# State-space chunks in quarter steps, six leading half tiles, and latent attention with hi and lo apart

## The chip, the core and the metric

The kernel runs on one core of a Trainium2 chip. The metric is the device time of one execution in microseconds (us); the core works with TensorE (matrix products, PE in the rows), VectorE (DVE), ScalarE (ACT), GpSimd (POOL) and the DMA queues, of which SP's carries most transfers.

## What is computed

Two stacks of layers on 512 positions of 1024 features, in float32. The first has two layers of a feed-forward block, a mixer, another feed-forward block and a gated embedding; the change doesn't touch it. The second has four branches, each between two norms: a state-space branch, a window attention, a latent attention and a gating unit (SGU).

```python
def s5_branch(h, ...):            # 64 groups of 16 channels, 64 states each
    u, z = split(h @ w_in)
    bu = einsum('blgh,gph->blgp', u, b)             # complex
    s = scan(a, bu)                                 # s[t] = a * s[t-1] + bu[t]
    y = gelu(real(einsum(s, c)) + d_skip * u)
    y = y * sigmoid(y @ w_glu + b_glu)
    return (y * silu(z)) @ w_out

def mla_branch(h, ...):           # 16 heads
    c_q, c_kv, k_rope, z = split(h @ w_in)          # 768, 256, 32, 1024
    q = rmsnorm(c_q) @ w_uq                         # 96 a head, 32 of them rotated
    k, v = rmsnorm(c_kv) @ w_ukv                    # 64 + 64 a head
    o = causal_softmax(q k^T) @ v
    return (o * silu(z)) @ w_out

x = x + rmsnorm(branch(rmsnorm(x)))
```

## The kernel before

Activations lie transposed: a tile is 128 features x 512 positions. Every float32 operand of a product is kept as two parts, hi and lo, and a product is three matmuls, hi x hi, hi x lo and lo x hi, into one PSUM bank (`mm3`, L446). A tile of a projection (`mtile`, L460) is up to 8 k steps of `mm3`. Weights come in units of 8 blocks of 128 x 128 (512 KB) by SP's queue into three buffers (`_dma`); `_split` (L394) makes hi on ScalarE and lo on VectorE, two units ahead of their use. Units of the four output projections are kept in SBUF slots, since they are used twice.

The order of the work is written out by hand. After k steps 2, 4 and 6 of a tile, and once after the tile, the program calls `fine` (L572) or `step` (L556); `step` counts a tick, advances the generators in `bgs`, and then calls `fine`, which runs what `soon` has put off and advances the generators in `fines`. So a generator in `bgs` moves twice a tile and one in `fines` four times, a quarter tile apart. All engines take their instructions in the order of this program. `split_soon` (L616) puts off the lo half of a split to the next `fine`, `split` (L605) does both at once; `join` (L635) copies one half of a product's rows on ScalarE and later adds the other on VectorE.

`lead` (L475) starts a projection whose last operands are not ready: it does the first `a` k steps of `m` tiles one tile after the other, calling `fine` after each second k step and `step` after each tile, and then one k step after the other for all `m` tiles, waiting for the operand where needed. Each tile in it had its own bank, and later tiles of the lead held their look-ahead of weight splits back (`hold`). `post_out` (L1265) is the output projection of a branch with the norm behind it, by halves of 256 positions: the first half of all 8 tiles with a lead of 3 half tiles and OUT_LEAD[i] k steps (state-space, window, latent, SGU), then the second half with the kept weights.

The state-space stage (`s5`, L1559): 16 tiles of the input projection (u, then z); each u tile goes through DRAM by two SP DMAs into another layout. The generator `ssm` (L1624) works on 8 chunks: `scan_in` (L1574, TensorE products, two ScalarE copies out of the same bank, eight VectorE operations with the scan among them), `scan_out` (L1598, TensorE products, a copy, two SP DMAs through DRAM) and `finish` (L1614, the skip term, gelu and split into the operand of the GLU projection). In `bgs`, steps half a tile apart: chunks 3 apart, lags 3, 6 and 10. Tables for the scan come by POOL's queue two chunks ahead (`tabs`, L1546).

The latent attention (`mla`, L1877): `latent` makes the compressed operands; then for 8 pairs of heads come two query tiles of 6 k steps, one key tile of 2 k steps, and for every second pair four pieces of V in two banks (`split_v`). The key tile's halves are copied by SP DMAs to the heads' key slots, and a pair is `ready` three ticks later. `causal` (L1049), a generator in `fines`, does for each head scores, exp, divide, transposes (`turn`), their lo parts and the product with V (`pv`), at lags of 9, 10, 11 and 13 calls; heads start at least 4 calls apart. V's hi and lo stood packed in one operand of 128 columns for a head, so `pv` was two matmuls a block (`mm2`, L455) and its result had to be joined from two halves of the rows.

## Time and profile before

| | |
|---|---|
| median of 3 runs | 3344.68 us (3342.61 to 3346.49) |
| the profiled execution | 3344.01 us |
| its span | 3342.2 us |
| TensorE, VectorE, ScalarE, GpSimd busy | 97%, 63%, 39%, 13% |
| mean granted TensorE clock | 0.988 |

The stages of the second stack lie at about 2318 to 2500 us (state-space and GLU), 2500 to 2565 (its output projection), 2565 to 2720 (window attention), 2720 to 2790 (its output projection), 2790 to 3027 (latent operands and attention), 3027 to 3140 (output projection, the first part with the last heads beside it) and 3140 to 3342 (SGU). An engine's idle time matters where it is TensorE's, and the releaser named beside a wait is the instruction that ended it. L248 is the line through which all VectorE instructions go, so these are told apart by their tiles and shapes.

### The profile page before, as it was taken

Reading aid. Unit: us, or ns where it says so; the run is one execution under the profiler, and the core shown is the slowest. Engines: PE = TensorE matmul, PEld = TensorE weight load, DVE = VectorE, ACT = ScalarE, POOL = GpSimd, SP = SyncE. Lnnn points to the kernel's source line nnn. Section 1 sums busy time; section 2 is a strip of 40 time slices with the busy share of each in tenths; the row PEclk is TensorE's granted clock in tenths of the full one; section 3 lists DMA queues with packets and bytes.
Section 4 is the critical chain, followed back from the end, with each engine's and each line's share of the span. In section 5 each row is a group of like instructions: output and inputs, shape, how many; then the busy total and the mean of one; then the engine's idle time right before and its main releaser. Section 6 shows DMA issues by size and latency. Waiting matters only on the chain. (4 is left out here: it accounts for less than half of the span.)

```text
span 3342.2 us, 42393 instructions
## 1 busy us (share of the span) xinstructions
PE 3249.7 (97%) x15832; PEld 2704.9 (81%) x15832; DVE 2107.2 (63%) x4096; ACT 1313.9 (39%) x2242; POOL 440.8 (13%) x558
## 2 busy tenths in 40 slices
PE   9999999999999999999999999999999899998997
PEld 7888777888888888887778888887879788877887
DVE  6653488766653676536887654347665876676665
ACT  4322334433322333323434423234444764455432
POOL 0100013001100011000220000001103332143201
PEclk9999999999999999999999999999999999998998
DMA  5433221224432334332222332334623122322221
GB/s 179 134 113 101 88 95 64 95 89 136 140 119 95 94 130 139 114 99 91 89 64 95 106 119 95 119 127 150 210 91 105 58 77 83 108 66 64 82 82 64
DMA packets 120302, 348.08 MB, mean 104 GB/s; under 512 B 30560, under 2 KB 33280, under 8 KB 120096
## 3 DMA queue, kind: packets, MB, share of 16 engines
q1 hardware_dynamic: 103824, 295.68, 27.7%
q0 software_dynamic: 16272, 49.69, 4.4%
q8 instruction: 125, 2.05, 0.2%
q14 instruction: 81, 0.66, 0.1%
HBM read 312.75 MB, written 28.11 MB: 102 GB/s over the span
## 5 line engine op out<-in xcount | busy, mean ns | idle before, releaser
L450 PE MATMUL mm<-s,whi 128*128 128x512 f32 (+1 forms) x3528 | 1381.0, 391 | 17.0 <-ACT s L777 7.1
L452 PE MATMUL mm<-s,wlo 128*128 128x512 f32 (+1 forms) x3528 | 1364.0, 387 | 5.9 <-DVE wlo L248 5.9
L451 PE MATMUL mm<-s,whi 128*128 128x512 f32 (+1 forms) x3528 | 1364.8, 387 | 3.7 <-DVE s L248 3.3
L248 DVE TENSOR_TENSOR wlo<-raw,whi 128x1024 fp32r<-128x1024 f32 (+1 forms) x488 | 594.0, 1223 | 534.3 <-ACT whi L407 530.8
L450 PEld LDWEIGHTS mm<-s,whi 128*128 128x128 f32 x3528 | 665.8, 189 | 151.8 <-ACT s L777 7.5
L452 PEld LDWEIGHTS mm<-s,wlo 128*128 128x128 f32 x3528 | 665.0, 188 | 144.9 <-DVE wlo L248 9.9
L451 PEld LDWEIGHTS mm<-s,whi 128*128 128x128 f32 x3528 | 665.9, 189 | 134.9 <-DVE s L248 8.2
L407 ACT CAST whi<-raw 128x1024 fp32r<-128x1024 f32 (+1 forms) x488 | 508.1, 1045 | 557.6 <-PE mm L451 275.8
L248 DVE TENSOR_TENSOR s<-s,s 128x512 f32<-128x512 f32 (+8 forms) x920 | 454.5, 519 | 147.4 <-ACT s L608 77.7
L248 DVE TENSOR_TENSOR s<-mm,rbc 128x512 f32<-128x512 f32 x296 | 199.6, 686 | 193.4 <-PE mm L452 172.2
L1081 POOL TENSOR_SCALAR s<-s,m 128x128 f32<-128x128 f32 (+3 forms) x128 | 157.1, 1233 | 502.0 <-DVE m L248 292.8
L248 DVE SCALAR_TENSOR_TENSOR s<-s,vecs,s 128x511 f32<-128x511 f32 (+13 forms) x256 | 181.3, 749 | 4.9 <-DMA s<-yd 3.0
L608 ACT CAST s<-s 128x512 fp32r<-128x512 f32 (+1 forms) x125 | 75.4, 613 | 266.3 <-DVE s L248 266.3
L884 ACT ACTIVATE s<-s 128x512 f32<-128x512 f32 x88 | 55.6, 632 | 251.6 <-DVE s L248 251.6
L450 PE MATMUL mm<-s,s 128*128 128x256 f32 x448 | 131.7, 294 | 11.8 <-ACT s L618 5.1
L777 ACT ACTIVATE s<-h,vecs 128x512 fp32r<-128x512 f32 (+1 forms) x112 | 70.9, 633 | 182.4 <-DVE h L248 182.4
L451 PE MATMUL mm<-s,s 128*128 128x256 f32 x448 | 129.7, 289 | 1.3 <-DVE s L248 1.0
L452 PE MATMUL mm<-s,s 128*128 128x256 f32 x448 | 129.2, 288 | 0.2 <-DVE s L248 0.2
L248 DVE TENSOR_TENSOR s<-sd,s 128x512 fp32r<-128x512 f32 (+5 forms) x186 | 93.9, 530 | 54.1 <-ACT s L1089 36.0
L248 DVE SCALAR_TENSOR_TENSOR s<-h,vecs,s 128x512 fp32r<-128x512 f32 (+1 forms) x112 | 80.5, 721 | 65.9 <-ACT s L777 65.9
L450 PE MATMUL sd<-s,whi 128*128 128x512 f32 x296 | 120.7, 408 | 0.9 <-ACT whi L407 0.9
L452 PE MATMUL sd<-s,wlo 128*128 128x512 f32 x296 | 116.2, 393 | 2.8 <-DVE wlo L248 2.8
(216 smaller groups left out, 3402.9 us busy)
## 6 DMA issues: line engine op xcount, KB each, us to landing
raw<-in_mix_dram SPq DMA_DIRECT2D x104, 512.0 KB, 3.5
raw<-in_ff2i_dram SPq DMA_DIRECT2D x88, 512.0 KB, 3.5
raw<-in_ff1i_dram SPq DMA_DIRECT2D x87, 512.0 KB, 3.6
raw<-in_ff1o_dram SPq DMA_DIRECT2D x44, 512.0 KB, 3.5
raw<-in_ff2o_dram SPq DMA_DIRECT2D x44, 512.0 KB, 3.5
raw<-in_mlaw_dram SPq DMA_DIRECT2D x33, 512.0 KB, 3.5
tab<-s POOLq DMA_DIRECT2D x64, 256.0 KB, 2.3
s<-tab POOLq DMA_DIRECT2D x64, 256.0 KB, 5.7
```

What stands on the lines that cost most here:

```text
L248: return f(*a, **kw)
L407: self.nc.scalar.copy(hi.bitcast(F32R), src)
L450: mm(ps, wh, xh, start=first, stop=False)
L451: mm(ps, wh, xl, start=False, stop=False)
L452: mm(ps, wl, xh, start=False, stop=last)
L608: nc.scalar.copy(hi.bitcast(F32R), src)
L777: self.nc.scalar.activation(hi.bitcast(F32R), src, AF.Copy, scale=gv)
L884: nc.scalar.activation(sg, ta, AF.Silu)
L1081: nc.gpsimd.tensor_scalar(out=pr[:, c], in0=pr[:, c], scalar1=ri, scalar2=None, op0=ALU.mult)
```

## The change

- The state-space generator moves from `bgs` to `fines`; chunks are 5.5 quarter steps apart (alternately 5 and 6). `scan_in` is cut in three: the products, copies and the first vector product (lag 7), two vector operations and the scan with two copies (8), the turn back with three operations (9); scan-out follows at 13, finish at 20. The next tables are asked for after the third part.
- In `lead` with a column range, two half tiles share a bank (only the first matmul in a bank starts it), and the look-ahead of weight splits isn't held back. `post_out` leads with 6, 6, 6 and 3 half tiles, by 5, 6, 5 and 4 k steps, and takes its 8 result slots one by one.
- In the latent attention V's hi and lo are two operands, each with the 128 columns of two heads; `pv` is `mm3`, 12 matmuls a head instead of 8, and only the head's own 64 rows of the result are used, without a join. V's four pieces are split one a call. `split` takes the place of `split_soon` for latent, query, key and result tiles.

```diff
-S5_LAGS = 10, 6, 3, 3
+S5_LAGS = 20, 13, 9, 8, 7
+S5_STEPS = 5.5
-OUT_LEAD = 4, 6, 4, 4
+OUT_LEAD = 5, 6, 5, 4
+OUT_TILES = 6, 6, 6, 3
@@ lead
+        banks = [self.mm() for _ in range((m + 1) // 2)] if c is not None else []
...
-                x, o = (x[0][:, c], x[1][:, c]), o[:, :c.stop - c.start]
-            self.mm3(o, w[j][k], x, k == 0, k == nk - 1)
+                x = x[0][:, c], x[1][:, c]
+            self.mm3(o, w[j][k], x, k == 0 and (c is None or j % 2 == 0), k == nk - 1 and (c is None or j % 2 == 1 or j == m - 1))
         for j in range(m):
-            pss.append(self.mm())
-            w.append([self.block(hold=j * nk // UB) for _ in range(nk)])
+            pss.append(self.mm() if c is None else banks[j // 2][:, j % 2 * 256:(j % 2 + 1) * 256])
+            w.append([self.block(hold=j * nk // UB if c is None else 0) for _ in range(nk)])
@@ post_out
-        ys = self.slots(KD)
+        ys = []
...
+                if e == 0:
+                    ys.append(self.slot())
...
-        for m, ps in enumerate(self.led(M, KD, KD, 3, halves[0], OUT_LEAD[i])):
+        for m, ps in enumerate(self.led(M, KD, KD, OUT_TILES[i], halves[0], OUT_LEAD[i])):
@@ s5
-            vt, x, m8 = self.slot(), self.slot(), M8.pop(m)
-            c, s = a[2:]
+            vt, x = self.slot(), self.slot()
...
+            S[m] = vt, x
+
+        def scan(m):
+            (vt, x), m8, s = S[m], M8[m], tables[m][0][3]
             v.tensor_tensor(g3(x)[:, :, 1:], g3(x)[:, :, 1:], g3(s)[:, :, 1:], op=ALU.mult)
             v.tensor_tensor(g3(vt)[:, :, 1:], g3(vt)[:, :, 1:], g3(x)[:, :, 1:], op=ALU.add)
             v.tensor_tensor_scan(x, m8, vt, 0.0, op0=ALU.mult, op1=ALU.add)
             for r, q in ((top, bot), (bot, top)):
                 nc.scalar.copy(m8[r], x[q])
-            v.tensor_tensor(vt, x, c, op=ALU.mult)
-            v.scalar_tensor_tensor(out=m8, in0=m8, scalar=-1.0, in1=s, op0=ALU.mult, op1=ALU.mult)
+
+        def turned(m):
+            (vt, x), m8, a = S[m], M8.pop(m), tables[m][0]
+            v.tensor_tensor(vt, x, a[2], op=ALU.mult)
+            v.scalar_tensor_tensor(out=m8, in0=m8, scalar=-1.0, in1=a[3], op0=ALU.mult, op1=ALU.mult)
             v.tensor_tensor(vt, vt, m8, op=ALU.add)
             self.free(m8, x, a)
             S[m] = vt
@@ ssm
-            d = S5_LAGS[3]
-            for k in range(d * (KD - 1) + S5_LAGS[0] + 1):
-                while len(UG) <= min(k // d, KD - 1):
+            jobs = {}
+            for m in range(KD):
+                for n, (f, lag) in enumerate(zip((finish, scan_out, turned, scan, scan_in), S5_LAGS)):
+                    jobs.setdefault(int(S5_STEPS * m) + lag, []).append((n, f, m))
+            for k in range(max(jobs) + 1):
+                while len(UG) <= min(int(k / S5_STEPS), KD - 1):
                     yield
...
+                for _, f, m in sorted(jobs.get(k, []), key=lambda x: x[0]):
+                    f(m)
+                    if f is turned:
+                        self.tabs(m + 1 + S5_AHEAD)
...
-                self.bgs.append(bg)
+                self.fines.append(bg)
@@ mla
-                    self.split_soon(t, hi, lo, self.vec(gname, m), lambda: (self.free(t), out.append((hi, lo))))
+                    self.split(t, hi, lo, self.vec(gname, m))
                     self.stat_add(st, t)
+                    self.free(t)
+                    out.append((hi, lo))
...
-            w = [x[:, c].bitcast(F32R) for x in V[h // 4]]
+            vh, vl = self.r(V[h // 4])
+            c = [slice(j % 2 * 256 + p % 2 * P, j % 2 * 256 + (p % 2 + 1) * P) for j in range(4)]
             def epi():
-                t = self.slot()
-                def rest():
-                    v.tensor_tensor(Z[p][rows], Z[p][rows], t[rows], op=ALU.mult)
-                    self.free(t)
-                    if h % 2:
-                        x = self.slot(), self.slot()
-                        self.split_soon(Z[p], *x, None, lambda: (self.free(Z[p]), M.append(x)))
-                self.join(t[rows], po, rest)
+                v.tensor_tensor(Z[p][rows], Z[p][rows], po[rows], op=ALU.mult)
+                if h % 2:
+                    M.append((self.slot(), self.slot()))
+                    self.split(Z[p], *M[p])
+                    self.free(Z[p])
...
-                         lambda h: None, score, values, MLA_LAGS, self.mm2)
+                         lambda h: None, score, values, MLA_LAGS, self.mm3)
...
-                    for src, two, r in xs:
-                        nc.scalar.activation(two[:, 0].bitcast(F32R), src, AF.Copy, scale=r)
-                    for i, (src, two, r) in enumerate(xs):
-                        if i % 2 == 0:
-                            yield
-                        v.scalar_tensor_tensor(out=two[:, 1].bitcast(F32R), in0=src, scalar=r, in1=two[:, 0],
-                                               op0=ALU.mult, op1=ALU.subtract)
+                    for i in range(4):
+                        yield
+                        c = slice(i % 2 * 256, (i % 2 + 1) * 256)
+                        self.split(vps[i // 2][:, c], hl[0][i // 2][:, c], hl[1][i // 2][:, c],
+                                   box["kvc"][:, i:i + 1])
...
-                    self.split_soon(t, hi, lo, None, lambda: self.free(t))
+                    self.split(t, hi, lo)
+                    self.free(t)
...
-                def rest():
-                    while len(scored) < 2 * p - 2:
...
-                self.split_soon(t, *tt, None, rest)
+                self.split(t, *tt)
+                while len(scored) < 2 * p - 2:
+                    self.fine()
+                for h in (2 * p, 2 * p + 1):
+                    for a, b in zip(KS[h % 4], tt):
+                        nc.sync.dma_start(a[nope(h)], b[nope(h)])
+                    ready[h] = self.tick
+                self.free(t, tt)
```

## Rows read from the trace of the kernel before

**Rows 1.** The page, busy time, share of the span and instructions of TensorE first.
```profile
PE 3249.7 (97%) x15832; PEld 2704.9 (81%) x15832; DVE 2107.2 (63%) x4096; ACT 1313.9 (39%) x2242; POOL 440.8 (13%) x558
```

**Rows 2.** Windows by stretch: length, busy us of each engine, granted clock, DMA.
```profile
core 0: us, PE busy (x) PEld busy (x) DVE busy (x) ACT busy (x) POOL busy (x), PEclk, DMA share, GB/s
2318.00:2381.80 63.80, 59.11 (x343) 51.48 (x341) 39.20 (x59) 32.05 (x42) 9.96 (x19) 1.00 0.77 237
2381.80:2395.40 13.60, 13.60 (x56) 12.63 (x55) 9.12 (x13) 4.46 (x7) 3.72 (x7) 0.50 0.74 263
2395.40:2446.60 51.20, 47.66 (x282) 41.65 (x280) 37.09 (x53) 23.66 (x37) 3.72 (x7) 1.00 0.39 118
2446.60:2460.30 13.70, 13.25 (x46) 11.58 (x47) 5.00 (x7) 3.70 (x6) 0.00 (x0) 0.50 0.29 93
...
2920.00:3027.40 107.40, 98.24 (x547) 83.52 (x547) 82.34 (x216) 63.96 (x153) 46.21 (x40) 1.00 0.25 70
3027.40:3071.20 43.80, 34.70 (x198) 28.79 (x197) 31.05 (x84) 24.48 (x62) 19.62 (x17) 0.92 0.13 36
3071.20:3081.50 10.30, 7.24 (x30) 6.66 (x31) 5.99 (x10) 6.07 (x14) 1.46 (x2) 0.50 0.28 89
```

**Rows 3.** Timeline, TensorE, state-space stage: start, length, line, form, [idle before <- releaser].
```profile
2327.65 1.97 PE L1578 MATMUL sd<-s,s 128*128 128x64 f32 x16 [2.26 <-DMA s<-ud]
...
2381.39 0.43 PE L1606 MATMUL sd<-s,s 128*128 128x64 f32 x2 [2.23 <-DVE s L248]
...
2447.05 0.80 PE L450 MATMUL mm<-s,whi 128*128 128x512 f32 x1 [3.90 <-ACT s L618]
```

**Rows 4.** Timeline, ScalarE and VectorE: the stalled chunk's copies and first product.
```profile
2374.10 1.17 ACT L1584 COPY s<-sd 64x504 f32<-64x504 f32 x2
2375.30 0.68 DVE L248 TENSOR_TENSOR s<-sd,s 128x504 f32<-128x504 f32 x1 [2.34 <-ACT s L1584]
```

**Rows 5.** Timeline, TensorE, latent attention: a head's pv, then a projection's products.
```profile
3019.27 1.45 PE L458 MATMUL sd<-s,s 128*128 128x512 f32 x8
3020.56 0.40 PE L450 MATMUL mm<-s,whi 128*128 128x512 f32 x1
3020.79 0.40 PE L451 MATMUL mm<-s,whi 128*128 128x512 f32 x1
```

**Rows 6.** Windows, a stretch of half-width products only.
```profile
2755.00:2775.25 20.25, 20.25 (x171) 20.22 (x170) 12.54 (x25) 10.24 (x29) 8.67 (x12) 1.00 0.01 2
```

**Rows 7.** Timeline, latent attention: V's pieces, a head's join, the second query tile.
```profile
2944.45 1.56 ACT L1993 ACTIVATE s<-mm,m 128x256 fp32r<-128x256 f32 x4
...
2946.04 0.58 ACT L637 COPY s<-sd 64x512 f32<-64x512 f32 x1
...
2947.64 0.87 DVE L248 SCALAR_TENSOR_TENSOR s<-mm,m,s 128x256 fp32r<-128x256 f32 x2
...
2948.56 0.50 PE L450 MATMUL mm<-s,whi 128*128 128x512 f32 x1 [0.62 <-DVE s L248]
...
2949.95 0.67 DVE L248 TENSOR_TENSOR s<-s,sd 64x512 f32<-64x512 f32 x1
```

**Rows 8.** Waits of TensorE, 3027.4 to 3088: us in total, times, longest.
```profile
PE mm L450 <- ACT s L618: 4.8, 2, 2.8
PE sd L458 <- DVE s L248: 3.6, 8, 1.2
```

**Rows 9.** Timeline, SGU's end: a kept unit's lo, a result's products, its split, TensorE.
```profile
3271.09 1.28 DVE L248 TENSOR_TENSOR s<-raw,s 128x512 fp32r<-128x512 f32 x2
...
3276.60 1.98 DVE L248 SCALAR_TENSOR_TENSOR s<-sd,vecs,s 64x256 f32<-64x256 f32 x4
...
3280.04 0.69 DVE L248 TENSOR_TENSOR s<-s,s 128x512 fp32r<-128x512 f32 x1 [0.74 <-ACT s L608]
3280.06 0.39 PE L450 MATMUL mm<-s,s 128*128 128x256 f32 x1 [2.23 <-ACT s L608]
```

**Rows 10.** The page, DMA issues: engine, count, size, median us to landing.
```profile
raw<-in_mlaw_dram SPq DMA_DIRECT2D x33, 512.0 KB, 3.5
```

More of the change, by code (lines that the diff above doesn't have):

```diff
@@ L1624, in ssm @@
         def ssm():
-            d = S5_LAGS[3]
-            for k in range(d * (KD - 1) + S5_LAGS[0] + 1):
-                while len(UG) <= min(k // d, KD - 1):
-                    yield
-                for f, lag in zip((finish, scan_out, scan_in), S5_LAGS):
-                    m, odd = divmod(k - lag, d)
-                    if odd == 0 and 0 <= m < KD:
-                        f(m)
-                        if f is scan_in:
-                            self.tabs(m + 1 + S5_AHEAD)
+            jobs = {}
[4 more added lines that the diff above has]
+                while len(UG) <= min(int(k / S5_STEPS), KD - 1):
+                    yield
+                for _, f, m in sorted(jobs.get(k, []), key=lambda x: x[0]):
+                    f(m)
+                    if f is turned:
+                        self.tabs(m + 1 + S5_AHEAD)
                 yield
@@ L1955, in values @@
         def values(h, po):
-            p, rows = h // 2, self.HALVES[h % 2]
-            c = slice(h % 4 * P, (h % 4 + 1) * P)
-            w = [x[:, c].bitcast(F32R) for x in V[h // 4]]
+            p, r0 = h // 2, 64 * (h % 2)
+            rows = slice(r0, r0 + 64)
+            vh, vl = self.r(V[h // 4])
+            c = [slice(j % 2 * 256 + p % 2 * P, j % 2 * 256 + (p % 2 + 1) * P) for j in range(4)]
             def epi():
-                t = self.slot()
-                def rest():
-                    v.tensor_tensor(Z[p][rows], Z[p][rows], t[rows], op=ALU.mult)
-                    self.free(t)
-                    if h % 2:
-                        x = self.slot(), self.slot()
-                        self.split_soon(Z[p], *x, None, lambda: (self.free(Z[p]), M.append(x)))
-                self.join(t[rows], po, rest)
+                v.tensor_tensor(Z[p][rows], Z[p][rows], po[rows], op=ALU.mult)
[3 more added lines that the diff above has]
+                    self.free(Z[p])
                 if h % 4 == 3:
                     self.free(V.pop(h // 4))
-            return epi, w
+            return epi, [(vh[j // 2][:, c[j]], vl[j // 2][:, c[j]]) for j in range(4)]
         bg = self.causal(16, lambda h: h in ready and self.tick >= ready[h] + 3, lambda h: True,
-                         lambda h: None, score, values, MLA_LAGS, self.mm2)
+                         lambda h: None, score, values, MLA_LAGS, self.mm3)
         self.fines.append(bg)
@@ L1985, in mla, with split_v @@
                                  (KVr[k][0][:, c], KVr[k][1][:, c]), w[k], k == 0, k == 1)
-                vs = self.slots(4)
-                def split_v(vps=vps, vs=vs):
-                    xs = [(vps[i // 2][:, i % 2 * 256:(i % 2 + 1) * 256].rearrange("p (h c) -> p h c", h=4),
-                           vs[i].rearrange("p (h b c) -> p b h c", h=4, b=2), box["kvc"][:, i:i + 1])
-                          for i in range(4)]
-                    for src, two, r in xs:
-                        nc.scalar.activation(two[:, 0].bitcast(F32R), src, AF.Copy, scale=r)
-                    for i, (src, two, r) in enumerate(xs):
-                        if i % 2 == 0:
-                            yield
-                        v.scalar_tensor_tensor(out=two[:, 1].bitcast(F32R), in0=src, scalar=r, in1=two[:, 0],
-                                               op0=ALU.mult, op1=ALU.subtract)
+                hl = (self.slots(2), self.slots(2))
+                def split_v(vps=vps, hl=hl):
+                    for i in range(4):
[3 more added lines that the diff above has]
+                                   box["kvc"][:, i:i + 1])
                 self.fines.append(split_v())
-                V[p // 2] = vs
+                V[p // 2] = hl
             for h in (2 * p, 2 * p + 1):
@@ L2015, in epi @@
                 tt = (self.slot(), self.slot())
-                def rest():
-                    while len(scored) < 2 * p - 2:
-                        self.fine()
-                    for h in (2 * p, 2 * p + 1):
-                        for a, b in zip(KS[h % 4], tt):
-                            nc.sync.dma_start(a[nope(h)], b[nope(h)])
-                        ready[h] = self.tick
-                    self.free(t, tt)
-                self.split_soon(t, *tt, None, rest)
+                self.split(t, *tt)
[6 more added lines that the diff above has]
+                self.free(t, tt)
             self.after_tile(epi)
-        self.settle()
         self.free(*CQ, *CKV, tEO)
```

2 lines of the change are left out of this document (1 added, 1 removed).

## The prediction

> **What bounds the kernel now.** I read the page's busy line first: TensorE is busy 97% of the span, so nearly all of its time is matmul work that the change leaves alone [rows 1]. What can be won is TensorE's idle time and the stretches in which its clock was granted at half, and what can be lost is added matmul work. The windows by stretch come next; in them compare the length of a stretch with the first number (TensorE busy) and read PEclk (1.00 is 2.4 GHz, 0.50 is 1.2 GHz). In the state-space stage two stretches, 13.6 and 13.7 us long, ran at 0.50 with TensorE busy almost throughout, and in the latent attention (MLA) 9.2 us are idle up to 3027.4 and 12.2 us from there to 3081.5, the last 10.3 us at 0.50 [rows 2]. The instructions in order of time then name what ended each idle stretch in the state-space stage: 2.26 us for the first chunk's DMA, 2.23 us in front of a chunk's scan-out, which waited for VectorE, and 3.90 us in front of the gate projection (GLU), which waited for the sixth chunk's result on ScalarE. Each of the last two comes just before a half-clock stretch [rows 2, 3]. So a wait there costs its own length and about as much again: half of a busy stretch at 0.50 is lost, 13.60/2 = 6.8 us and 13.25/2 = 6.6 us.
>
> **Units.** Two full-width products start 0.23 us apart [rows 5]. A quarter tile is six of them, 1.38 us. A chunk's scan-in takes 1.97 us on TensorE [rows 3]; its scan-out has twice as many products, so about 3.9 us (an estimate from the same row). The half-width products of the output projections take 20.25/171 = 0.12 us [rows 6].
>
> **State-space chunks.** Work is neither added nor removed: the same products, vector operations, table loads and DMAs, in another order. Before, a chunk's scan-out stands six quarters behind its scan-in with nothing else of the scan in between: 8.3 us. In the row of the stalled chunk ScalarE's copies of the scan-in came late, VectorE's first product began behind them, and TensorE waited 2.23 us [rows 3, 4]. After, scan-in, scan-out and the distance of chunks are 7, 13 and alternately 5 and 6 quarters. Where the next chunk follows after 5, its scan-in (1.97 us) falls between; where it follows after 6, the scan-out of the chunk before (3.9 us) does. The allowance is 10.2 or 12.2 us, so the shortfall of 2.23 us is covered or leaves 0.3 us. The stalled chunk is the fourth, whose successor follows after 6 quarters: covered. Its half-clock stretch I take to go with the wait: 2.23 + 6.8 = 9.0 us.
>
> At the end of the stage the finishing step of the sixth chunk stood in VectorE's queue behind the whole scan of the eighth. After, the eighth's scan-in and scan are issued in quarters 45 and 46, the sixth's finish in 47, and its result is first read after 6 + 24 + 15 products and the eighth's scan-out: 45 x 0.23 + 3.9 = 14.2 us later, against 27 x 0.23 = 6.2 us before (12 products of the tile, 15 of the lead). The wait was 3.90 us, so it fits: 3.90 + 6.6 = 10.5 us. The eighth's finish comes in quarter 58, where GLU's lead now also advances the chunks (before, once a tile), so its result stands ahead of the last of GLU's eight k steps. The first wait of 2.26 us shrinks by one quarter, 1.38 us. Together 9.0 + 10.5 + 1.4 = 20.9 us. Four of the eight chunks have the short allowance, up to 0.3 us each, and VectorE is busy 37.1 of 51.2 us here [rows 2] in a loop that gets tighter: a chunk takes 5.5 x 1.38 + 1.97 + 3.9 = 13.5 us of TensorE against 14.2. I take off 2.9 us: **-18 us**, from -22 to -1.4 (only the first wait).
>
> The queues passed: SP carries the same pairs of DMAs through DRAM for each tile and chunk, in the same order, because the write of a scan-out stays behind the DMAs of the same tiles; the result has 7 quarters before it is finished and had 8. The table loads on POOL are asked for behind the third part instead of the first, 14.5 quarters before they are read and not 18; 14.5 x 1.38 us are 20 us even without the scan's products, against 3.5 us for a transfer of twice the size of one [rows 10]. Both cost nothing as long as that holds; without it a chunk waits up to 3.5 us.
>
> **Six leading half tiles.** Their number of products is the same; what changes is that the first three output projections cover a late operand with 6 x 5 or 6 x 6 k steps instead of 3 x 4 or 3 x 6, and that the weight splits are no longer held back in the lead. A held unit costs VectorE 1.28 us when it is split [rows 9]. Behind the state-space stage the wait is for such a split, which stays queued behind GLU's last result: 0, from -1.3 to +1.3. In the window attention the extra splits enter VectorE's queue in front of the last heads; two of them, one half regained by the wider cover: +1.3 us, from -1.3 to +2.6. In the gating unit (SGU) the lead stays at 3 x 4 but loses the hold too. There VectorE works without pause for four results, 1.98 us of products each with a wait of 0.74 us, and TensorE waits 2.23 us for the third of them [rows 9]; two splits come in between: 2 x 1.28 = **+2.5 us**, from 0 to +4 if the clock suffers.
>
> **Latent operands apart.** The probability-value product of a head took 8 matmuls of a packed hi and lo, 3019.27 to 3020.56, 1.29 us [rows 5]. With three products instead of two it takes 12: +0.645 us, and 16 heads give **+10.3 us** of TensorE time. In exchange ScalarE loses a copy of 0.58 us and VectorE an addition of 0.67 us for each head [rows 7], on engines that were not the bound but that TensorE waits for. The split of V now goes piece by piece: ScalarE's four pieces of 1.56 us and VectorE's pairs of 0.87 us [rows 7] are spread over four calls instead of three, and the second query tile, which already waited 0.62 us for its bank [rows 7], gets it one call later. A call spans a quarter tile and a share of a head's matmuls, over 2 us; VectorE is ahead by what it no longer does. I take +1.0 us for each of the three V units that lie inside the attention, +3 us, from -1.9 (the wait goes) to +7.2 (a call and the wait's own pace, 2.4 us each).
>
> Here a rule of the Trainium skill is weighed. VectorE's first product of a chunk waited for ScalarE's two copies, which it doesn't read: they only read the same PSUM bank [rows 4]. "PSUM — Partial Sum Buffer", section "PSUM bank collisions raise a hardware error", says that two engines must not touch one bank and quadrant at once, and that a scheduler therefore orders even two readers. The trace agrees. By it the two V pieces in one bank are handed over ScalarE, VectorE, ScalarE, VectorE, and the bank's wait lies at its upper end, 7.2 us instead of 3: 4 us later in all.
>
> Query and key tiles: the split now follows in the same queue position, and a pair of heads is called ready one step earlier, which is two calls. Its key copies on SP get two calls less, where a transfer of 512 KB took 3.5 us [rows 10]; between 0 and 3.5 us at a pair, I take 0, since five calls are left.
>
> What is regained: up to 3027.4 TensorE idles 107.40 - 98.24 = 9.2 us; 0.65 us more of its own work and 0.67 us less of VectorE's in each head make it late for half of these waits: -4.6 us. From 3027.4 to 3081.5 it idles 9.1 + 3.1 us and loses to the clock 0.16 x 43.8/2 x 0.79 = 2.8 and 7.24/2 = 3.6 us [rows 2]: 18.6 us, and the waits are for the last results on ScalarE and for VectorE in front of the heads' products [rows 8]. Before, 9 calls run under the lead, 3 x 3, and 17 of the rest have no tile work beside them. After, the last pair starts three calls earlier, its result needs two fewer, the lead has 18 calls and two k steps more, and four bare calls are left. The 63 further half products put 63 x 0.12 = 7.6 us into the waits, and the bare calls go from 17 to 4. I leave 3.3 us for these and 5 us for the covered ones: 8.3 of 18.6 us, -10.3 us. MLA in sum: 10.3 + 3 - 4.6 - 10.3 = **-1.6 us**, from -13 to +13.3 (nothing regained). The latents' own split before it changes only the order of two vector operations: 0.
>
> **Sum.** The profiled execution took 3344.0 us, span 3342.2 and 1.8 around it, and the median of the runs shown is 3344.7, so both stand for the same. -18 + 0 + 1.3 - 1.6 + 2.5 = -15.8: **3328 us**.
>
> **The rivals.** *The tail hides all*: the lead covers MLA's last heads, MLA -13, the state-space stage -20: 3344.0 - 33 + 3.8 = 3315. For it speaks that TensorE's waits are many and short; against it, that they stand in front of single heads' products, which no half tile is next to. *The scan stays bound by its queue*: VectorE takes the shorter loop badly, one of the two stalls GLU's wait, returns: -18 + 10.5 = -7.5 there, 3339. *The third product is bare*: MLA +13.3 and the rest as forecast: 3343; for it speaks that up to 3027 the clock is full and TensorE busy 91% [rows 2]. *Slower*: one mechanism, VectorE's strict order as the real bound in both stages. Its place is the chunk loop and the attention loop; its price is that neither stall goes (-1.4 left) and that nothing pays for the products (+13.3), with 3.8 for the splits: 3360. It decides from the point at which VectorE's busy time and the waits that it sits out, now 37.1/51.2 of 14.2 us, 10.3 us a chunk, and waits such as one of 2.34 us [rows 2, 4], pass 13.5 us a chunk. *V's pieces take turns at their bank*: the second query tile waits for four hand-overs, 7.2 instead of 3 us: 3332; for it speaks the wait on the copies [rows 4], against it that a call now parts the pieces.
>
> **How the numbers follow.** Forecast 0.40 (its own range 3318 to 3337), V's turns 0.08, tail hides all 0.20, scan stays bound 0.13, product bare 0.10, slower 0.09. A measurement tells 0.2%, 6.7 us, from no change: below 3338 is faster. The forecast, V's turns, the covered tail and 0.04 of the scan's case lie there: 0.72; the rest of that case and the bare product are within: 0.19; slower 0.09. The range takes in all but the slower case and the far end of the covered tail: 3308 to 3345.
>
> **What would show it.** Right: no half clock between 2380 and 2460, scan-out not waiting over 0.5 us, GLU's lead running through; 12 products a head in about 1.9 us; the last pair's scores during the second leading half tile; SGU's two waits longer by 1.3 us each. Wrong: a new wait in front of scan-ins or for a chunk's result, a half-clock stretch in MLA before 3027 (a bank wait of 2 us could be followed by one), or a tail as long as before.

## The result

The changed kernel takes **3327.08 us** (median, 3325.52 to 3329.92) against 3343.64 for the kernel before: a ratio of 0.9949 with a 95% interval of 0.9936 to 0.9961. The forecast was 3328, range 3308 to 3345. The sum was right; two of its terms were far off, in opposite directions.

The page's busy line of the profiled run (3325.52 us, span 3323.7), which answers to [rows 1]: TensorE has 64 instructions more, 4 for each of 16 heads, and is busy 5.7 us less.

```profile
PE 3244.0 (98%) x15896; PEld 2705.2 (81%) x15896; DVE 2097.4 (63%) x4080; ACT 1305.0 (39%) x2226; POOL 437.7 (13%) x558
```

**State-space stage.** The windows by stretch, columns as in [rows 2]: the half-clock stretch behind GLU's wait is gone (granted clock 1.00 from 2396.00 on), but the one at 2382 is still there, 13.7 us long. A further one of 6.8 us, from 2341.4, is what takes the first window to 0.95.

```profile
2318.00:2382.30 64.30, 59.55 (x330) 51.99 (x328) 39.09 (x58) 31.84 (x43) 9.83 (x19) 0.95 0.68 214
2382.30:2396.00 13.70, 12.51 (x52) 11.96 (x53) 6.12 (x11) 4.35 (x7) 2.91 (x6) 0.50 0.78 266
2396.00:2444.00 48.00, 48.00 (x300) 42.85 (x298) 39.11 (x56) 24.09 (x37) 4.25 (x8) 1.00 0.37 122
2444.00:2463.00 19.00, 18.80 (x86) 15.29 (x84) 7.33 (x9) 6.87 (x10) 0.00 (x0) 1.00 0.25 83
```

The instructions of TensorE in order of time, as in [rows 3]: the first chunk's scan-in and GLU's lead no longer wait. Instead the first chunk's scan-out waits 1.15 us, and the fourth's, which waited 2.23, now waits 4.79.

```profile
2339.09 0.43 PE L1618 MATMUL sd<-s,s 128*128 128x64 f32 x2 [1.15 <-DVE s L250]
...
2383.49 0.69 PE L1618 MATMUL sd<-s,s 128*128 128x64 f32 x2 [4.79 <-DVE s L250]
```

VectorE in order of time ahead of that wait (the fourth chunk's scan-in ends on TensorE at 2366.69): its first product at 2370.94; a gate's operations up to 2374.2; the scan at 2375.61; then 2.44 us idle for the hi half of a weight split, the split's lo, the second chunk's finish, and only then the third part, from 2381.42.

```profile
2370.94 0.67 DVE L250 TENSOR_TENSOR s<-sd,s 128x504 f32<-128x504 f32 x1
...
2375.61 1.23 DVE L250 TENSOR_TENSOR_SCAN s<-s,s 128x512 f32<-128x512 f32 x1
2379.28 1.22 DVE L250 TENSOR_TENSOR wlo<-raw,whi 128x1024 fp32r<-128x1024 f32 x1 [2.44 <-ACT whi L409]
2380.42 1.08 DVE L250 SCALAR_TENSOR_TENSOR s<-s,vecs,s 128x512 f32<-128x512 f32 x1
2381.42 0.69 DVE L250 TENSOR_TENSOR s<-s,s 128x512 f32<-128x512 f32 x1
```

ScalarE at the same time: the weight's hi stands behind the scan's two copies, which wait for the scan; and the chunk's own two copies (L1589) came 2.5 us after the scan-in, behind a table load, a gelu and a weight's hi.

```profile
2365.11 1.28 ACT L1632 ACT_TABLE_LOAD   x1
...
2368.11 1.04 ACT L409 CAST whi<-raw 128x1024 fp32r<-128x1024 f32 x1
2369.17 1.16 ACT L1589 COPY s<-sd 64x504 f32<-64x504 f32 x2
...
2376.93 1.25 ACT L1600 COPY s<-s 64x512 f32<-64x512 f32 x2 [2.91 <-DVE s L250]
2378.20 1.04 ACT L409 CAST whi<-raw 128x1024 fp32r<-128x1024 f32 x1
```

**Latent attention.** TensorE's waits from the last rotation DMA to the first tables of SGU (us in total, times, longest): all that is left of what [rows 8] showed two waits of is one of 1.5 us for the last result, and the granted clock is 1.00 throughout.

```profile
PE sd L452 <- DVE s L250: 2.5, 4, 1.2
PE mm L452 <- DVE s L250: 2.1, 2, 1.3
PE mm L452 <- ACT s L612: 1.5, 1, 1.5
PE sd L452 <- ACT whi L409: 1.4, 1, 1.4
```

A head's pv has 12 matmuls, from 3011.26 to 3013.18: 1.92 us, against 1.29 in [rows 5].

**The stages in numbers.** The same instructions were sought in both traces (the first copy of a u tile, GLU's last tanh, the window attention's first exp, the first DMA of the latent attention, SGU's last table DMA, the last output DMA). The table gives, in us against the profiled run of before, what each stretch between them gained or lost, for the changed kernel and for all experiments. "Window" and "latent" hold their stage with its output projection's lead; SGU is from its tables on. Each line is one profiled execution; mla_two's, join_back's and gelu_later's took longest of theirs. Stretches of identical code differ by up to 2.9 us here (ahead, in gelu_later), so 3 us in a single line are no finding. Where several kernels share the code of a stage, they count together:

- state space: the six with the changed order gain 6.0 to 8.9 us;
- window attention: the seven with six half tiles behind it lose 2.6 to 3.5 us, the six others change by -0.3 to +0.8;
- SGU: the six without the hold lose 1.4 to 2.9 us, the seven others change by -0.6 to +0.1.

| kernel | ahead | state space, GLU | its projection | window | latent | SGU | sum |
|---|---|---|---|---|---|---|---|
| changed kernel | -0.8 | -7.1 | -2.0 | +3.0 | -13.2 | +1.4 | -18.7 |
| s5_only | +0.3 | -6.4 | -0.3 | +0.7 | -1.5 | -0.1 | -7.2 |
| mla_only | -0.5 | +1.7 | 0 | -0.3 | -9.0 | -0.6 | -8.7 |
| lead_only | -0.5 | +2.1 | -0.7 | +3.0 | +0.6 | +2.9 | +7.4 |
| mla_split | +0.4 | -0.3 | 0 | +0.1 | +1.4 | -0.6 | +0.9 |
| mla_two | -0.4 | -8.9 | -2.1 | +3.5 | -15.7 | +2.6 | -21.0 |
| join_back | +0.9 | -6.0 | -0.7 | +3.0 | +3.4 | +2.0 | +2.7 |
| s5_whole | -0.4 | -10.0 | -0.8 | +2.6 | -13.1 | +2.9 | -18.9 |
| s5_lag15 | +0.9 | -4.6 | -1.7 | +2.8 | -13.0 | +2.6 | -13.1 |
| gelu_later | +2.9 | -9.5 | 0 | +0.8 | -11.3 | -0.1 | -17.2 |
| two_parts | +0.5 | -7.6 | +0.3 | +0.2 | -12.7 | -0.3 | -19.6 |
| hold | 0 | -6.6 | -1.7 | +3.5 | -12.5 | -0.1 | -17.4 |
| lead_6363 | +0.1 | -8.9 | -2.0 | +0.5 | -12.9 | +0.1 | -23.2 |

Forecast against the first line: state space -18, its projection 0, window +1.3, latent -1.6, SGU +2.5.

### The profile page after: what moved, and what is told of

It is laid out like the page before. It is cut to its first block, busy times and chain, and to the rows that moved or that the text cites. A ratio compares the mean times of both kernels' runs of the same rounds, so it can differ in the third digit from the quotient of the medians.

```text
span 3323.7 us, 42450 instructions
## 1 busy us (share of the span) xinstructions
PE 3244.0 (98%) x15896; PEld 2705.2 (81%) x15896; DVE 2097.4 (63%) x4080; ACT 1305.0 (39%) x2226; POOL 437.7 (13%) x558
## 4 chain that ended last, share of the span: by engine, by line
PE 84%; DVE 9%; ACT 4%; issue 3%; DMA 0%; SPq 0%; DVEq 0%; ACTq 0%
PE mm L452 23%; PE mm L454 23%; PE mm L453 23%; DVE s L250 6%; PE sd L452 4%; PE sd L454 3%; PE sd L453 3%; DVE wlo L250 1%; ACT whi L409 1%; PE sd L1092 1%; DVE h L250 1%; DVE m L250 1%; PE sd L460 1%; PE sd L734 1%; PE sd L701 1%
## 5 line engine op out<-in xcount | busy, mean ns | idle before, releaser
L250 DVE TENSOR_TENSOR s<-s,s 128x512 f32<-128x512 f32 (+7 forms) x904 | 443.2, 516 | 132.9 <-ACT s L612 100.1
L612 ACT CAST s<-s 128x512 fp32r<-128x512 f32 x157 | 95.3, 615 | 316.5 <-DVE s L250 316.5
L452 PE MATMUL sd<-s,s 128*128 128x256 f32 (+4 forms) x352 | 118.6, 337 | 4.2 <-DVE s L250 2.5
```

Of the source, the lines that this page charges most:

```text
L250: return f(*a, **kw)
L452: mm(ps, wh, xh, start=first, stop=False)
L612: nc.scalar.copy(hi.bitcast(F32R), src)
```

## The experiments

### Each part of the change alone

From the diff shown above: s5_only has the hunks of `s5`, mla_only those of `mla`, lead_only those of `lead` and `post_out`, each on the kernel before.

> The kernel before with the state-space part of the change alone (quarter steps, chunks 5.5 apart, the scan in three). The prediction's term for it: -18 us, 3326, with no half clock between 2380 and 2460. What the trace of the changed kernel suggests instead: GLU's wait and its half-clock stretch are gone, but the fourth chunk still stalls in front of its scan-out (4.8 us, then 13.65 us at half clock), so the stage brings 8 to 10 us: 3334 to 3336. If the leads or the latent attention had a part in the stage's gain, it would be nearer to 3344.

> The kernel before with the latent attention's part alone (V's hi and lo apart, three products, splits in one go), the leads as before (3 half tiles, 4 k steps, hold). Theory A, that the lead hides the tail: without it the tail's regained 10.3 us are missing from my -1.6, so +8.7: 3352. Theory B, that the attention was bound by VectorE's and ScalarE's queue and gains from the joins that went: it keeps most of the 13 us that the stage gained in the changed kernel, -8 to -13: 3331 to 3336, and the third product is hidden.

> The kernel before with the leading half tiles alone (6, 6, 6, 3 of them, no hold). The prediction's terms without the latent attention's: 0 + 1.3 + 2.5, and what a wider lead covers of the tail there, -10.3 or less: 3337 to 3348. Theory A (the lead hides the tail): window attention +3, SGU +2, the tail -10: 3339. Theory B (VectorE's queue): the tail keeps its waits, 3348.

Measured: s5_only 3336.35 us, ratio 0.9974 (0.9964 to 0.9984); mla_only 3335.45, 0.9974 (0.9965 to 0.9984); lead_only 3351.29, 1.0020 (1.0010 to 1.0029). So -8.3, -9.2 and +6.7 against 3344.63 in the same runs: together -10.8, where the whole change brings 16.6. The state-space part is worth about what the changed kernel's trace suggested (3334 to 3336) and not 18. In s5_only the fourth chunk's scan-out waits 2.57 us, 14.6 us after its scan-in and behind the same operations; 4.79 us is the changed kernel's figure (3.92 in hold, 4.82 in lead_6363), so the state-space part by itself leaves the stall about as long as it was. The latent attention gains by itself and without the wider lead, as theory B had it. The lead costs where it stands alone, 3 us more than even theory B's 3348; with the new attention the latent stage gains another 4.2 us (-13.2 against -9.0), which neither theory foretold.

### What the latent attention gains from

mla_split is the kernel before with the splits of the latent, query and key tiles alone; the result tiles, which its text names too, are still split behind the join. The hunk of the query tiles, of three:

```diff
-                    self.split_soon(t, hi, lo, None, lambda: self.free(t))
+                    self.split(t, hi, lo)
+                    self.free(t)
...
```

> The kernel before with one piece of the latent attention's change: latent, query, key and result tiles are split at once instead of half a quarter later; V stays packed, with two products and the join. The latent part alone brought 9.2 us. If the gain came from the splits (a pair ready two calls earlier, the last heads earlier), this keeps 8 us or more, since the third product is not in it: 3326 to 3337. If it came from the joins that went and V apart, this brings nothing: 3342 to 3346.

Measured: 3345.53 us, ratio 1.0003 (0.9993 to 1.0012). Nothing, so the gain is in what is left: V apart, the third product, the join that went, and the result tiles split at once. The next two leave out the third product and give the join's work back, both from the changed kernel.

```diff
-                         lambda h: None, score, values, MLA_LAGS, self.mm3)
+                         lambda h: None, score, values, MLA_LAGS,
+                         lambda po, w, x, a, b: (self.pe(po.shape[-1], 1), self.mm2(po, w[0], x, a, b)))
```

> The changed kernel with two of the three products in the heads' pv: V's lo times the probabilities is left out, so 8 matmuls a head instead of 12, and the output is a little less exact. It measures the third product by itself. The prediction's term, 16 x 0.645 = 10.3 us, if TensorE is the bound throughout: 3317. Rival: with TensorE quicker, VectorE and ScalarE are late again in front of the heads' products, and part or all of it turns into waits (the prediction took half back): 3320 to 3327.

```diff
-                v.tensor_tensor(Z[p][rows], Z[p][rows], po[rows], op=ALU.mult)
+                t = self.slot()
+                nc.scalar.copy(t[rows], po[rows])
+                def rest():
+                    v.tensor_tensor(t[rows], t[rows], po[rows], op=ALU.max)
+                    v.tensor_tensor(Z[p][rows], Z[p][rows], t[rows], op=ALU.mult)
...
+                self.soon(rest)
```

> The changed kernel with the join's work given back to each head: a ScalarE copy of 64x512 out of the pv result and, at the next call, a VectorE operation of 64x512 with it (a maximum with itself, so nothing changes), then the gate product; V stays apart with three products. Theory: what pays for the third product is that ScalarE and VectorE lost this work (0.58 + 0.67 us a head, 20 us in all): most of the 8 us that the third product does not cost come back as waits: 3334 to 3341. Rival: the third product fills TensorE's waits by itself, or the order of V's pieces made them: 3327 to 3330.

Measured: mla_two 3321.18 us, ratio 0.9929 (0.9914 to 0.9944); 5.9 us quicker than the changed kernel by the medians, 2.3 by the two profiled executions, in which the latent stage is 2.5 us quicker (-15.7 against -13.2). join_back 3342.14 us, ratio 0.9992 (0.9983 to 1.0002), a little over the theory's 3334 to 3341: 15 us slower than the changed kernel by the medians, 21 by the profiled executions, of which 16.6 lie in the latent stage. So 16.6 is an upper end. The windows of that stage from the last rotation DMA on, one line each for before, the changed kernel, mla_two and join_back (length, TensorE busy, ..., granted clock):

```profile
2829.32:3123.70 294.38, 273.06 (x1561) 237.05 (x1560) 198.78 (x473) 154.57 (x347) 91.17 (x86) 0.97 0.27 78
```

```profile
2821.97:3103.54 281.57, 272.62 (x1626) 240.84 (x1625) 189.18 (x457) 145.43 (x331) 87.07 (x86) 1.00 0.27 81
```

```profile
2820.98:3100.15 279.17, 267.50 (x1562) 234.92 (x1561) 187.82 (x457) 145.24 (x331) 86.76 (x86) 0.98 0.28 82
```

```profile
2826.21:3124.42 298.21, 279.96 (x1626) 245.32 (x1625) 198.67 (x473) 154.62 (x347) 86.76 (x86) 0.98 0.26 77
```

Idle is the length less TensorE's busy time: 21.3 before, 9.0 in the changed kernel, 11.7 without the third product, 18.3 with the join's work. So without the third product TensorE waits 2.7 us longer and half clock comes back (10.2 us of it): of the 10.3 us of the products, this execution shows 2.4 in the length, 2.7 turn into waits, and the other 5 go with the clock. With the join's 16 copies and 16 operations given back (9.2 us of ScalarE, 9.5 of VectorE, by the fourth and third busy column) 9.3 us of idle return, and half clock with them (13.6 us). The order of V's pieces stayed as changed in both, so it isn't what pays by itself. One thing join_back doesn't separate: as with the join before, each head's result also comes a call later and its bank is held for as long. By it the waits for results (`mm`, ScalarE) grow from 1.5 to 2.9 us and those in front of the heads' products (`sd`, VectorE) from 3.4 to 11.1; what of this is the engines' time and what the later call wasn't tested.

### What the scan-outs wait for

s5_whole puts the scan in one part, from the changed kernel; s5_lag15 adds two quarters; gelu_later and two_parts go from lead_6363 (below). In all four the next tables are asked for behind the part that the scan's end now stands in.

```diff
-S5_LAGS = 20, 13, 9, 8, 7
+S5_LAGS = 20, 13, 7       # s5_whole: scan_in, scan and turned in one call
+S5_LAGS = 21, 15, 7       # s5_lag15: the same
+S5_LAGS = 20, 13, 8, 7    # two_parts: scan and turned in one call
```

> The changed kernel with the scan in one part again (all of it with the scan-in, lag 7), chunks and lags of scan-out (13) and finish (20) as in the change. Theory: the fourth chunk's stall is made by the three parts, since weight splits, a gate's operations and the second chunk's finish come between them in VectorE's queue (16.7 us from the end of scan-in to the last operation, against 7.9 before): in one part it ends in about 8 us, the allowance of 10.2 to 12.2 holds, and the stall of 4.8 and the 6.8 of its half clock go: 3315. Rival: it is the tighter distance of chunks and VectorE's load, whatever the parts: a stall of 2 us or more stays, 3324 to 3330.

> The changed kernel with the scan in one part and two quarters more from scan-in to scan-out (lags 7, 15, 21). With one part and 13, waits of 0.57, 2.71 and 0.37 us were left at the fourth, fifth and eighth chunk's scan-out: two quarters are 2.76 us, so all go, and the half-clock stretch of 10.2 us behind the second of them: 3.7 + 5 us less than that kernel's 3328: 3320. Rival: scan-out waits for what VectorE and ScalarE do in strict order, and these run later too (the result is finished a quarter later, so GLU's lead waits for it again, up to 3.9 us and a half-clock stretch of 13.7 us): 3328 to 3335.

Measured: s5_whole 3328.51 us, ratio 0.9951 (0.9936 to 0.9966), state-space stage -10.0 instead of -7.1: the fourth chunk waits 0.57 us, but now the fifth waits 2.71, with a half-clock stretch of 10.2 us. The theory held for the fourth chunk and not for the stage; the time lies in the rival's range (3324 to 3330). s5_lag15 3330.80 us, ratio 0.9958 (0.9943 to 0.9972), -4.6: with 2.76 us more the fifth chunk waits longer still, 3.64, and GLU's lead waits again (2.61). Too little distance is therefore not the cause at the fifth chunk; the time lies in the rival's range here too (3328 to 3335). VectorE's waits between 2380 and 2392 in s5_lag15 show what held the fifth chunk there: the second chunk's finish waited 3.9 us for a DMA, and the fifth chunk's first product stood behind it. SP's queue shows why: the read of a u tile (L1654) was issued 10.4 us after its write (L1652), as soon as that had landed, and the scan-out's write (L1615) stood behind it.

```profile
DVE s L250 <- DMA s<-yd: 3.9, 1, 3.9
```

```profile
2367.57 0.37 SPq L1652 DMA_DIRECT2D ud<-s  x1
2377.99 0.32 SPq L1654 DMA_DIRECT2D s<-ud  x1
2378.40 0.38 SPq L1615 DMA_DIRECT2D yd<-s  x1
2381.82 0.37 SPq L1616 DMA_DIRECT2D s<-yd  x1
```

gelu_later also puts the scan in one part and the gelu off by a quarter:

```diff
-            nc.scalar.activation(U[m], U[m], AF.Gelu_apprx_tanh)
-            self.split_soon(U[m], hi, lo, None, lambda: Y.append((hi, lo)))
...
+            def rest():
+                nc.scalar.activation(U[m], U[m], AF.Gelu_apprx_tanh)
+                self.split_soon(U[m], hi, lo, None, lambda: Y.append((hi, lo)))
+            self.soon(rest)
```

> The kernel with 6, 3, 6, 3 half tiles and the hold, the scan in one part (lags 7, 13, 20), and finish's gelu put off to the next quarter, so that it no longer stands in ScalarE's queue waiting for VectorE's product just in front of it (2.3 us each in the trace) with the next chunk's copies behind it. Theory: the strict order of the two queues makes the stalls: the fifth chunk's 2.71 us and its half clock (5.1 us) go, and with 4.4 us from the leads: 3328.5 - 4.4 - 7.8 = 3316. Rival: the copies then wait behind something else in the same queue (a gate's tanh, a weight split): 3322 to 3326.

> The kernel with 6, 3, 6, 3 half tiles and the hold, and the second and third part of the scan joined again (lags 7, 8, 13, 20): the scan and the turn back are issued without a break. In the three parts the fourth chunk's last operations stood behind a weight split whose hi ScalarE made only after the scan's copies (VectorE idle 2.44 us), the split's lo (1.23) and the second chunk's finish (1.08). Theory: this break makes the stall of 4.8 us at the fourth chunk; without it the last operation ends about 4 us earlier, the stall is 1 us or less, the 1.15 us of the first chunk go too, and so does some of the half clock behind them (13.7 us long): 3321.4 - 5 - 0 to 6.8 = 3310 to 3316. Rival: it is the copies, late in ScalarE's queue, and what the joined parts gain is lost at the next chunk, as with the scan in one part: 3319 to 3324.

Measured: gelu_later 3322.79 us, ratio 0.9933 (0.9917 to 0.9948), state-space stage -9.5, with waits of 1.16 us at the second chunk and 1.93 at the fifth; two_parts 3325.26 us, 0.9939 (0.9926 to 0.9953), -7.6, with 3.24 at the fourth and 1.17 at the eighth. gelu_later came out as its rival (3322 to 3326), two_parts above both its theory and its rival (3319 to 3324). In two_parts VectorE's row shows the fourth chunk's delay in another place, ahead of the scan: the first product (0.67 us) is behind a weight split that waits 3.76 us for its hi, and that stood on ScalarE behind the table load, the gelu and its split.

```profile
2369.06 1.22 DVE L250 TENSOR_TENSOR wlo<-raw,whi 128x1024 fp32r<-128x1024 f32 x1 [3.76 <-ACT whi L409]
2370.20 0.69 DVE L250 TENSOR_TENSOR s<-s,s 128x512 fp32r<-128x512 f32 x1
2370.82 0.67 DVE L250 TENSOR_TENSOR s<-sd,s 128x504 f32<-128x504 f32 x1
```

What follows: each of the five orders, the change's among them, has a wait of 1.9 to 4.8 us at the fourth or fifth chunk, each time behind something that VectorE or ScalarE takes in program order (a weight's split, a finish, a gate). In s5_whole and gelu_later, too, the fifth chunk's copies began 5.7 and 4.9 us after its scan-in, behind a gate's tanh and a weight's hi on ScalarE. The break between the parts is one such place and not the only one. By time the orders can't be ranked: -10.0, -9.5 and -7.6 lie in or next to the 6.0 to 8.9 us that the change's own order gains, and only s5_lag15 (-4.6) falls short. Which order has no such wait stays open.

### What the wider leads cost

Both from the changed kernel: hold gives the last two half tiles of each lead their hold back, lead_6363 also goes back to three half tiles behind the window attention.

```diff
-OUT_TILES = 6, 6, 6, 3
+OUT_TILES = 6, 3, 6, 3    # lead_6363 only
...
-            w.append([self.block(hold=j * nk // UB if c is None else 0) for _ in range(nk)])
+            w.append([self.block(hold=j * nk // UB if c is None else max(0, j - m + 3)) for _ in range(nk)])
```

> The changed kernel with the hold given back to the last two of the leading half tiles (0, 1 and 2 units for the last three, as before with three). The prediction: the window attention's and SGU's extra cost, 1.3 + 2.5 there and 2.9 + 1.5 in the traces, is that of the weight splits in front of the last results: it goes, 3322 to 3324. Rival: the splits only move behind the lead and the wider cover has no use for the rest; or the wider lead itself is what costs: 3327.

> The changed kernel with three leading half tiles again behind the window attention (6, 3, 6, 3), and the hold for the last two of each lead. A half tile consumes a whole weight unit, so six of them put three more units through ScalarE and VectorE beside the last heads; with the hold alone the window attention kept its +3 us and SGU lost its +1.5. Theory: it is the number of half tiles there, so the window attention's +2.9 and SGU's +1.5 both go: 3327.1 - 4.4 = 3322.7. Rival: the next lead or the clock gives it back: 3325 to 3328.

Measured: hold 3326.85 us, ratio 0.9946 (0.9932 to 0.9961); lead_6363 3321.37, ratio 0.9932 (0.9914 to 0.9950). With the hold SGU's loss goes (-0.1 instead of +1.4), the window attention's stays (+3.5), and the time is the one that the rival gave (3327); with three half tiles that goes too (+0.5), and the time is near the theory's (3322.7). TensorE's waits in front of SGU's results, first the changed kernel (before: 2.23 for the first, [rows 9]), then hold:

```profile
3261.08 0.58 PE L452 MATMUL mm<-s,s 128*128 128x256 f32 x1 [3.37 <-ACT s L612]
3266.45 0.58 PE L452 MATMUL mm<-s,s 128*128 128x256 f32 x1 [2.57 <-ACT s L612]
```

```profile
3262.79 0.38 PE L452 MATMUL mm<-s,s 128*128 128x256 f32 x1 [2.23 <-ACT s L612]
...
3266.96 0.58 PE L452 MATMUL mm<-s,s 128*128 128x256 f32 x1 [2.23 <-ACT s L612]
```

The last head's turn in the window attention, ScalarE of the changed kernel, then TensorE of it and of lead_6363: a weight's two hi halves stand directly in front of the casts that TensorE waits for.

```profile
2715.12 1.13 ACT L409 CAST s<-raw 128x512 fp32r<-128x512 f32 x2
2716.27 1.09 ACT L1820 CAST s<-sd 128x256 fp32r<-128x256 f32 x4
```

```profile
2716.70 0.49 PE L460 MATMUL sd<-s,s 128*128 128x256 f32 x1 [1.45 <-ACT s L1820]
```

```profile
2715.10 0.38 PE L460 MATMUL sd<-s,s 128*128 128x256 f32 x1 [0.54 <-ACT s L1820]
```

So it is the number of half tiles there: each takes the eight blocks of a whole weight unit for half the products, and six of them bring three more splits beside the last heads. The wait itself is longer by 0.9 us only; behind it the changed kernel runs 6.8 us at half clock:

```profile
2716.80:2723.60 6.80, 5.94 (x27) 5.65 (x28) 4.66 (x12) 3.19 (x9) 0.00 (x0) 0.50 0.29 100
```

Half of the 5.94 busy us are 3.0. All seven kernels with six half tiles have this second half-clock stretch (3.4 us long in s5_lag15), 10 to 14 us behind a first one, and none of the others has it. In SGU, likewise, the half-clock stretch at these waits is 10.2 us long in the six kernels without the hold and 6.8 in all others. So a good part of what the splits cost is clock. lead_6363's four executions (3320.82 to 3323.95) all take less than the changed kernel's four (3325.52 to 3329.92); by the stages in which it differs from it, it is 3.8 us ahead (2.5 in the window column, 1.3 in SGU's). The intervals of the two ratios still touch (0.9914 to 0.9950 and 0.9936 to 0.9961).

## Why the prediction was right

**State space, -18: too much by 11.** Right: GLU's lead runs through, and no half clock follows it (3.90 + 6.6 us); the first chunk's wait is gone (2.26, I had 1.4), in part by luck, since s5_whole, s5_lag15 and gelu_later, with the same lag, wait 1.57, 1.71 and 1.35 us there; a scan-out follows its scan-in by 10.1 to 11.9 us at five of the six chunks that don't wait (16.4 at the second). Wrong: "the shortfall of 2.23 us is covered", and with it the first thing that was to show the forecast right, no half clock between 2380 and 2460. The step that failed took the chain from scan-in to the turn back to be as long as before, 8.3 us and the stall of 2.2; at the fourth chunk it took 16.8. Cut in three, the chain has between its parts whatever the queues hold there. Its stall grew by 2.6 us instead of going (by 0.3 in s5_only), its half-clock stretch of 13.7 us stayed, and the first chunk's 1.15 us with half of a 6.8 us stretch (3.4) came on top. My allowance for a tighter loop was 2.9 us; for the -7.1 measured it would have had to be 20.9 - 7.1 = 13.8. "The scan stays bound by its queue" was the rival for it, worked out at another place: it had GLU's wait return, and that was the one cured.

**Latent attention, -1.6: too little by 11.6.** Right: 12 matmuls in 1.92 us a head, the third product itself (mla_two has 5.1 us less busy time although half clock lengthens it), and that the tail's waits go. What was mis-sized shows when the stage is divided at the last product of the last key tile, from the first DMA of the stage to SGU's tables, two lines each for before and the changed kernel:

```profile
2774.76:3026.64 251.88, 241.01 (x1273) 203.90 (x1272) 176.87 (x411) 128.38 (x265) 66.18 (x64) 1.00 0.31 89
3026.64:3123.70 97.06, 84.90 (x582) 78.14 (x581) 58.84 (x150) 49.72 (x124) 35.64 (x39) 0.91 0.20 57
```

```profile
2767.82:3023.92 256.10, 249.45 (x1335) 213.24 (x1334) 177.03 (x419) 128.29 (x266) 63.24 (x67) 1.00 0.29 90
3023.92:3103.54 79.62, 75.59 (x583) 72.28 (x582) 49.09 (x126) 40.68 (x107) 34.50 (x37) 1.00 0.21 63
```

Up to that product the stage is 4.2 us longer, where I had 10.3 + 3 - 4.6 = +8.7; the idle time there falls from 10.9 to 6.7, so the half that I took back, 4.6 us, was about right. Behind it the stage is 17.4 us shorter, where I had -10.3: I left 8.3 us of idle time and half clock, and 4.0 us of idle time are left and no half clock. The tail's step also had the wrong cause. Without the wider lead (mla_only) the part behind it is 83.2 us long, so 13.9 of the 17.4 us come without it, and no half clock is left either. With the join's work back (join_back) it is 90.9 us long, 11.2 more than in the changed kernel, and the part ahead 5.4 more: at most 16.6 us for the two small operations of a head and the later result, 1.0 us of TensorE a head, with the clock. What the lead adds is about 4 us, and only beside the relieved engines: alone it brings nothing (+0.6). The last pair's scores ran beside the third to fifth half tiles and not the second. V's pieces: a term of 3 us that measured 1.0 over all four units. The second query tile waited 1.26 and 0.89 us at the first two of V's units and not at the third and fourth; before it waited 0.62 and 0.57 us at the third and fourth and not at the first two. Pieces of one bank do take turns. ScalarE's hi of a unit's fourth piece waits 0.78 us for VectorE's lo of the third, which it doesn't read and which only lies in the same bank; VectorE then waits 0.54 us for that hi, which it does read. Each turn is about half a microsecond, and the rival's 7.2 us is not there:

```profile
2879.68 0.48 DVE L250 SCALAR_TENSOR_TENSOR s<-mm,m,s 128x256 fp32r<-128x256 f32 x1
2880.19 0.47 ACT L615 ACTIVATE s<-mm,m 128x256 fp32r<-128x256 f32 x1 [0.78 <-DVE s L250]
2880.70 0.48 DVE L250 SCALAR_TENSOR_TENSOR s<-mm,m,s 128x256 fp32r<-128x256 f32 x1 [0.54 <-ACT s L615]
```

**Leads.** SGU: +2.5 forecast, +1.4 measured and 2.0 to 2.9 in five other kernels with the same code, with the waits longer by 1.1 and 0.3 us instead of 1.3 each and 3.4 us more of half clock; the cause, the missing hold, is shown by hold. Window attention: +1.3 forecast with an end of 2.6, +3.0 measured. The step that failed weighed the extra splits against the wider cover, half regained; nothing was regained, a second half-clock stretch came on top, and the hold wasn't the cause. Behind the state-space stage: 0 forecast; -2.0 in the changed kernel and -1.7 to -2.1 in four experiments with that lead, -0.8 to +0.3 in the other five: within the spread, or a small gain.

**The sum.** -15.8 forecast, -18.5 in the span, because -18 for -7.1 and -1.6 for -13.2 nearly cancel. The range, 3308 to 3345, held by that luck as much as by its width. The slower rival, VectorE's order as the bound in both stages, was half true: the stalls left in the state-space stage stand behind it, and taking the join out of the two queues is what paid in the latent attention.

## What to carry to other kernels

Small operations on engines that feed TensorE in strict order can be worth more than the idle time seen beside them: two of 0.6 us a head, given back together with a result that came a call later, cost up to 1.0 us of TensorE a head here, clock included. Without them four extra matmuls a head cost 2.5 to 6 us in all and not 10.3. A slack reckoned from the schedule's distances holds only as long as the chain keeps its length; cut into parts, it takes in everything that the queues hold between them (16.8 us instead of 10.7 at the fourth chunk), and moving the reader later needs the same look at the DMA queues. Count the weight units that a lead consumes, not its products: half tiles double the splitting for each product, and here that cost showed as clock as much as in waits.

## What was not expected of the hardware

The granted clock fell to half behind waits of very different length, and not always: in the changed kernel 1.15 us at 2339.09 were followed by 6.8 us at half clock from 2341.4, while in lead_6363 the same wait at the same place (1.15 us, with 0.70 at the next scan-out) was followed by none before the stall of 4.8 us at 2382. So a stretch of half clock behind a wait of about 1 us can't be counted on in a sum, neither its coming nor its staying away. The other surprise was a u tile's write of 256 KB that landed 10.4 us after its issue (s5_lag15, 2367.57), with the DMA engines 74% busy between 2360 and 2380. In the kernel before, with them 80% busy between 2360 and 2381, the slowest of these writes took 7.8 us, so the load alone doesn't explain it, and the cause stays open.
